# Transposes of x moved inside the first product, one load of x set back, and a new way out for the last rows

## The chip, the cores and the metric

The kernel runs on one core of one Trainium2 chip. The metric is device time in microseconds, from launch to end, as the median of several runs. The engines of the core are named as the profile names them: PE is TensorE (matmuls; PEld is its weight load), DVE is VectorE, ACT is ScalarE, POOL is GpSimd, SP is SyncE, which here only issues transfers. Each engine has a queue of its own and works through it in order. Transfers (DMAs) are issued from the queues of SP, ACT and POOL and run on the core's 16 DMA engines. SBUF is the on-chip memory of 128 partitions, PSUM the eight banks into which PE writes.

## The reference

One step of a hybrid decoder layer, with a prompt of 256 rows and 8 samples of 8 rows (64 sample rows) that share the weights. The model width is 2048, all in float32.

```python
def decoder_layer(x, conv_prev, k_win, v_win, rel_bias, w_in, w_conv, w_conv_out, sinks,
                  w_attn_out, w_o, g_mix, g_ffn, w_gate, w_up, w_down):
    xn = rms_norm(x, g_mix)
    z = xn @ w_in                       # B | C | h | q | k | v | gate_conv | gate_attn
    ...
    u = c_gate * h_conv
    conv_out, conv_state = short_conv(u, conv_prev, w_conv)
    y_conv = (b_gate * conv_out) @ w_conv_out
    ...                                 # banded attention with a bias and a sink per head
    y_attn = attn @ w_attn_out
    merged = jax.nn.sigmoid(gate_c) * y_conv + jax.nn.sigmoid(gate_a) * y_attn
    h = x + merged @ w_o
    hn = rms_norm(h, g_ffn)
    h = h + (jax.nn.silu(hn @ w_gate) * (hn @ w_up)) @ w_down
    return h, conv_state, k_state, v_state
```

After the layer comes a final RMSNorm: each row of h is divided by the root of its mean square and multiplied by `g_final`. The outputs are `y_prompt` (256 x 2048), `y_sample` (64 x 2048) and the new key, value and convolution states, for which the sample caches are copied on, shifted by 8 rows.

## The kernel before

All 320 rows are handled together, transposed: a matrix of activations lies in SBUF as 16 chunks of 128 features by 320 rows. Every float32 product is made of three matmuls. Weights and activations are each split into a high part (`hi`, `xh`, rounded to the format of the fast matmul) and the rest (`lo`, `xl`), and hi x xh, hi x xl and lo x xh are added up in PSUM. A tile of weights comes in by one transfer from SP's queue into `wraw` (four buffers), ACT makes `whi` (L93) and DVE `wlo` (L94), with three buffers each.

The framework orders each engine's queue by itself, from what is ready in its own plan, with the order of the program as priority; it also sets all semaphores. `with after(mark):` adds one rule: the instructions inside are queued behind `mark` on the same engine. It is an order and not a wait for data.

**Start.** x is loaded as rows: two tiles of 128 prompt rows and one of 64 sample rows (`xs`), in five groups of columns (`XB`, 2, 2, 4, 4 and 4 chunks; `x_load(i)` issues three transfers, from SP's queue but for one). The first product (`kv_product`, L267) makes keys and values and transposes x on the way. It takes 16 chunks in nine tiles of weights, two of one chunk and seven of two, and four groups of 128 columns, c = 0 to 3, so that a chunk costs twelve matmuls. `x_prep(kc)` (L242) transposes chunk kc of the three row tiles on PE into one PSUM bank; then ACT writes `xh`, DVE writes `xl` and copies x to `hT`. The splits of a weight tile are queued behind the `xh` and `xl` of its first chunk (L263). Chunks 0 and 1 are prepared ahead of the products of chunk 0, chunks 2 and 3 ahead of those of chunk 1, and from chunk 2 on, chunk kc + 2 ahead of the products of chunk kc. The loads of x are issued behind those of weight tiles: group 1 behind tile 0, group 2 behind tile 1, group 3 behind tile 3, group 4 behind tile 4.

After each tile, `tick()` places a piece of side work (`start_rest`, L321): small loads on POOL, the squares of x on ACT (`squares`, L314, three activations a time, four times), and small transposes and matmuls on PE. The products that follow (`product`, L116) take two column groups at a time and all 16 chunks, four to a tile of weights.

Among the loads for the first of these, the query product, the sample caches are copied from memory to memory (L417), by two transfers from SP's queue of which each counts 8 samples outermost.

**End.** The last product (`dn`) adds to `hT`. In its second half each pair of chunks is transposed back to rows, into PSUM banks (`pc`, "fa"), one bank a chunk with three row tiles side by side. ACT squares them and adds up along the row (`row_squares`, L908, into `ssf`), DVE multiplies by `g_final` into `y_sb`. For the last pair the first chunk (`next_last`, L923) is treated while PE still works on the second; there DVE also sums the squares so far (`s15`, L932 and L933). The last chunk is added to `hT` and transposed in three pieces by row tile (L966 and L967), into one bank. Then, for row tile 0 and afterwards for tiles 1 and 2, the last squares, the mean (`row_mean`, L969), the root (`inv_root`, L181), the scaling of all columns, split between ACT and DVE, and the sends. Five sends of prompt rows go from SP's queue. Two sends of the sample rows (columns 0 to 767 and 768 to 2047, from 64 partitions) go from ACT's queue; the code's last lines are

```python
    with after(last["a"]):
        scale(nc.scalar, 2, r2, 0, 768)
    send(nc.scalar, 2, 0, 768)
    with after(last["y"]):
        last["y"] = scale(nc.vector, 2, r2, 768, e0)
    with after(last["y"]):
        scale_last(2, r2)
    send(nc.scalar, 2, 768, D)
```

## Time and profile before

| | us |
|---|---|
| median of 3 runs (1702.07 to 1702.84) | 1702.33 |
| the profiled execution | 1702.27 |
| its span | 1700.5 |
| PE busy | 1682.2 |
| DVE busy | 863.3 |
| ACT busy | 643.5 |
| mean granted clock of PE | 0.997 |

The span runs from the first to the last instruction that the profile shows; the device time holds a little more around it. In a row of the timeline the columns are start, duration, engine, line of the kernel, operation, output and inputs with their shapes, and a count; brackets hold the idle time of the engine before it and what ended that. `SPq` and `ACTq` are the queues that issue transfers. In a row of waits stand the one who waits, what it waited for, and the sum, the number and the longest of the waits. In a row of transfers stand the destination and source, the issuing queue, the count, the size of each and the median time from issue to landing. In a row of windows stand the stretch, its length, the busy time of PE, PEld, DVE, ACT and POOL with their instructions, the granted clock, the busy share of the DMA engines and GB/s. Matmuls are pipelined and their ends are modelled.

### The profile page before, as it was taken

The numbers are of one execution on the slowest core, as the hardware profiler recorded it, in microseconds if no ns is written. First come the engines' busy times: TensorE is split into PE (matmuls) and PEld (weight loads), VectorE is DVE, ScalarE is ACT, GpSimd is POOL, SyncE is SP. The second block draws the span as 40 slices with busy tenths as digits, with TensorE's granted clock in tenths as the row PEclk, the third lists the DMA queues.
The fourth block names the chain that finished last, engine by engine and source line by source line (L and its number), as shares of the span: only waits on it lengthen the run. The fifth ranks groups of instructions, "written<-read, shape, count | busy, mean of one in ns | idle before, by whom it ended". The sixth has DMA issues, their size and how long they took to land.

```text
span 1700.5 us, 27713 instructions
## 1 busy us (share of the span) xinstructions
PE 1682.2 (99%) x11600; PEld 1670.9 (98%) x11600; DVE 863.3 (51%) x1231; ACT 643.5 (38%) x945; POOL 81.3 (5%) x127
## 2 busy tenths in 40 slices
PE   8999999999999999999999999999999999999996
PEld 7999999999999999999999999999999999999996
DVE  7667554444444445556454545433345545454443
ACT  6445443333333333334333333322233333333432
POOL 1001221000000001220000000000000000000000
PEclk9999999999999999999999999999999999999998
DMA  7754554555555544444444444444444444445442
GB/s 217 216 153 142 161 151 131 147 150 151 151 152 151 149 149 149 149 149 149 149 149 150 149 150 152 152 152 150 149 150 149 149 149 149 149 151 171 149 140 96
DMA packets 256719, 258.22 MB, mean 152 GB/s; under 512 B 9091, under 2 KB 251615, under 8 KB 256433
## 3 DMA queue, kind: packets, MB, share of 16 engines
q1 hardware_dynamic: 254128, 249.86, 47.8%
q0 software_dynamic: 2128, 5.92, 1.2%
q8 instruction: 91, 1.49, 0.4%
q10 hardware_dynamic: 336, 0.66, 0.2%
q14 instruction: 36, 0.29, 0.1%
HBM read 253.29 MB, written 5.08 MB: 152 GB/s over the span
## 4 chain that ended last, share of the span: by engine, by line
PE 95%; issue 2%; DMA 1%; DVE 1%; SPq 0%; POOL 0%; ACT 0%; DVEq 0%; POOLq 0%; ACTq 0%
PE fg L134 18%; PE fu L134 18%; PE dn L134 18%; PE wo L134 7%; PE ga L134 7%; PE gc L134 7%; PE C L134 3%; PE B L134 3%; PE H L134 3%; PE ya L134 3%; PE yc L134 3%; PE q L134 2%; DMA wraw<-in_w_in_dram 0%; DMA rel<-in_rel_bias_dram 0%; PE po L508 0%
## 5 line engine op out<-in xcount | busy, mean ns | idle before, releaser
L94 DVE TENSOR_TENSOR wlo<-wraw,whi 128x1024 fp32r<-128x1024 f32 (+1 forms) x481 | 573.8, 1195 | 703.9 <-ACT whi L93 701.3
L93 ACT ACTIVATE whi<-wraw 128x1024 fp32r<-128x1024 f32 (+1 forms) x481 | 493.3, 1030 | 852.4 <-PE dn L134 198.2
L134 PE MATMUL dn<-a_h,whi 128*128 128x320 f32 x704 | 218.5, 310 | 0.0
L134 PE MATMUL fu<-hh_t,whi 128*128 128x320 f32 x704 | 217.4, 309 | 0.0
L134 PE MATMUL dn<-a_h,wlo 128*128 128x320 f32 x704 | 217.3, 309 | 0.0
L134 PE MATMUL dn<-a_l,whi 128*128 128x320 f32 x704 | 217.2, 309 | 0.0
L134 PE MATMUL fg<-hh_t,whi 128*128 128x320 f32 x704 | 217.2, 309 | 0.0
L134 PE MATMUL fg<-hl_t,whi 128*128 128x320 f32 x704 | 217.2, 309 | 0.0
L134 PE MATMUL fg<-hh_t,wlo 128*128 128x320 f32 x704 | 217.2, 309 | 0.0
L134 PE MATMUL fu<-hl_t,whi 128*128 128x320 f32 x704 | 217.2, 308 | 0.0
L134 PE MATMUL fu<-hh_t,wlo 128*128 128x320 f32 x704 | 217.2, 308 | 0.0
L134 PEld LDWEIGHTS fu<-hl_t,whi 128*128 128x128 f32 x704 | 132.2, 188 | 0.1
L134 PEld LDWEIGHTS dn<-a_l,whi 128*128 128x128 f32 x704 | 132.2, 188 | 0.0
L134 PEld LDWEIGHTS fu<-hh_t,whi 128*128 128x128 f32 x704 | 132.2, 188 | 0.1
L134 PEld LDWEIGHTS dn<-a_h,whi 128*128 128x128 f32 x704 | 132.2, 188 | 0.0
L134 PEld LDWEIGHTS dn<-a_h,wlo 128*128 128x128 f32 x704 | 132.2, 188 | 0.0
L134 PEld LDWEIGHTS fg<-hh_t,whi 128*128 128x128 f32 x704 | 132.2, 188 | 0.0
L134 PEld LDWEIGHTS fg<-hh_t,wlo 128*128 128x128 f32 x704 | 132.2, 188 | 0.0
L134 PEld LDWEIGHTS fg<-hl_t,whi 128*128 128x128 f32 x704 | 132.2, 188 | 0.0
L134 PEld LDWEIGHTS fu<-hh_t,wlo 128*128 128x128 f32 x704 | 132.2, 188 | 0.0
L134 PE MATMUL gc<-xh_t,whi 128*128 128x320 f32 x256 | 79.6, 311 | 0.0
L134 PE MATMUL ga<-xh_t,wlo 128*128 128x320 f32 x256 | 79.4, 310 | 0.0
(285 smaller groups left out, 2934.7 us busy)
## 6 DMA issues: line engine op xcount, KB each, us to landing
wraw<-in_w_in_dram SPq DMA_DIRECT2D x119, 512.0 KB, 3.6
wraw<-in_w_gate_dram SPq DMA_DIRECT2D x88, 512.0 KB, 3.6
wraw<-in_w_up_dram SPq DMA_DIRECT2D x88, 512.0 KB, 3.6
wraw<-in_w_down_dram SPq DMA_DIRECT2D x88, 512.0 KB, 3.5
wraw<-in_w_o_dram SPq DMA_DIRECT2D x32, 512.0 KB, 3.5
wraw<-in_w_in_dram SPq DMA_DIRECT2D x34, 256.0 KB, 4.4
wraw<-in_w_conv_out_dram SPq DMA_DIRECT2D x16, 512.0 KB, 3.5
wraw<-in_w_attn_out_dram SPq DMA_DIRECT2D x32, 256.0 KB, 4.1
```

The lines of the kernel that those rows point to most:

```text
L93: last["hi"] = nc.scalar.activation(hi, src, AF.Copy)
L94: last["lo"] = nc.vector.tensor_sub(lo, src, hi.bitcast(F32))
L134: last["mm"] = nc.tensor.matmul(ps[c][:, :T], w[:, k, c * P:(c + 1) * P], x(kc), start=(kc == 0 and i == 0), stop=(kc == nk - 1 and i == 2),)
```

## The change

At the start, chunks 0 and 1 are prepared ahead of the first load of weights in the program, and every later chunk kc + 2 is prepared at c = 3 of chunk kc, with its transposes queued behind the matmuls issued so far (those of c = 0 to 2). Group 2 of x is loaded behind weight tile 2 instead of tile 1.

At the end, the last chunk's three transposes go to three PSUM banks; the sum of the squares so far is made behind the last adds. The sample rows are scaled into a new tile `yo` of 128 partitions by 1024 columns: columns 0 to 1023 of row r in partition r, columns 1024 to 2047 in partition 64 + r. ACT scales the first half, DVE the second. Two sends take 512 columns each of all 128 partitions; the destination's access pattern counts 2 halves, 64 rows and 512 columns. All sends go from SP's queue. The tile `yb` becomes larger by 1024 columns.

```diff
--- before.py
+++ after.py
@@ -241,8 +241,9 @@
 
     def x_prep(kc):
         pt = ps_aux(u("pt"))
-        for t in range(3):
-            nc.tensor.transpose(pt[:, t * P:(t + 1) * P], xs[t][:, kc * P:(kc + 1) * P], ident)
+        with after(*((last["mm"],) if kc > 1 else ())):
+            for t in range(3):
+                nc.tensor.transpose(pt[:, t * P:(t + 1) * P], xs[t][:, kc * P:(kc + 1) * P], ident)
         m1 = nc.scalar.activation(xh_t[:, kc, :], pt[:, :T], AF.Copy, scale=g_mix[:, kc:kc + 1])
         m2 = nc.vector.scalar_tensor_tensor(
             xl_t[:, kc, :], pt[:, :T], g_mix[:, kc:kc + 1], xh_t[:, kc, :].bitcast(F32),
@@ -267,6 +268,8 @@
     def kv_product(tiles, x_after):
 
         ps = [ps_acc(u("kv")) for _ in range(4)]
+        x_prep(0)
+        x_prep(1)
         k0 = 0
         for i, n in enumerate(tiles):
             hi, lo = load_kv(k0, n)
@@ -277,9 +280,8 @@
                 order.sort(key=lambda kc: kc[1])
             for k, c in order:
                 kc = k0 + k
-                if c == 0:
-                    for j in range(2 * kc, 2 * kc + 2) if kc < 2 else range(kc + 2, min(kc + 3, KC)):
-                        x_prep(j)
+                if c == 3 and kc + 2 < KC:
+                    x_prep(kc + 2)
                 for m, (w, x) in enumerate(((hi, xh), (hi, xl), (lo, xh))):
                     last["mm"] = nc.tensor.matmul(
                         ps[c][:, :T], w[:, k, c * P:(c + 1) * P], x(kc),
@@ -363,7 +365,7 @@
         nc.vector.tensor_mul(rbsq, rb, rb)
 
     side_work[0] = start_rest()
-    ps_kv = kv_product([1, 1] + [2] * 7, {0: (1,), 1: (2,), 3: (3,), 4: (4,)})
+    ps_kv = kv_product([1, 1] + [2] * 7, {0: (1,), 2: (2,), 3: (3,), 4: (4,)})
     for _ in side_work[0]:
         pass
     for c in range(2):
@@ -897,9 +899,11 @@
                 split_to(a_h[:, fpair * 2 + c, :], a_l[:, fpair * 2 + c, :], gs[c])
         if half == 1:
             ya = xp.tile([P, 2, D], F32, tag="xh", name="ya")
-            yb = xp.tile([P, 2, D], F32, tag="xl", name="yb")
-            y_sb = [ya[:, 0, :], ya[:, 1, :], yb[:, 0, :]]
-            gfb = yb[:, 1, :]
+            yb = xp.tile([P, 2 * D + DC], F32, tag="xl", name="yb")
+            y_sb = [ya[:, 0, :], ya[:, 1, :], yb[:, 0:D]]
+            gfb = yb[:, D:2 * D]
+
+            yo = yb[:, 2 * D:]
             nc.gpsimd.dma_start(gfb, a["g_final"].partition_broadcast(P))
             ssf = op.tile([P, 3, KC], F32, name="ssf")
             nc.vector.memset(ssf, 1.0)
@@ -908,14 +912,21 @@
             def row_squares(t, k, pt):
                 tn = TOK[t][1]
                 jk = tmp("td", "jk")
-                nc.scalar.activation(
-                    jk[:tn, :P], pt[:tn, t * P:(t + 1) * P], AF.Square, accum_out=ssf[:tn, t, k:k + 1]
-                )
+                nc.scalar.activation(jk[:tn, :P], pt[t][:tn], AF.Square, accum_out=ssf[:tn, t, k:k + 1])
 
             def y_part(k, pt):
                 for t, (t0, tn) in enumerate(TOK):
                     ks = slice(k * P, (k + 1) * P)
-                    nc.vector.tensor_mul(y_sb[t][:tn, ks], pt[:tn, t * P:(t + 1) * P], gfb[:tn, ks])
+                    nc.vector.tensor_mul(y_sb[t][:tn, ks], pt[t][:tn], gfb[:tn, ks])
+
+            def to_rows(k, dst, tr=(0, 1, 2)):
+                for t in tr:
+                    t0, tn = TOK[t]
+                    nc.tensor.transpose(dst[t][:tn], hT[:, k, t0:t0 + tn], ident)
+
+            def one_bank():
+                pt = ps_aux(u("fa"))
+                return [pt[:, t * P:(t + 1) * P] for t in range(3)]
 
             warm = op.tile([P, 1], F32, name="warm")
             with after(last["sig"]):
@@ -923,14 +934,11 @@
         def next_last(ps):
 
             k = KC - 2
-            pc[0] = ps_aux(u("fa"))
+            pc[0] = one_bank()
             nc.vector.tensor_add(hT[:, k, :], hT[:, k, :], ps[0][:, :T])
-            for t, (t0, tn) in enumerate(TOK):
-                nc.tensor.transpose(pc[0][:tn, t * P:(t + 1) * P], hT[:, k, t0:t0 + tn], ident)
+            to_rows(k, pc[0])
             for t in range(3):
                 row_squares(t, k, pc[0])
-            nc.vector.tensor_reduce(s15, ssf[:, :, 0:KC - 1], axis=AX.X, op=ALU.add)
-            nc.vector.tensor_scalar(s15, s15, 1.0 / D, EPS, op0=ALU.mult, op1=ALU.add)
 
         pc = [None, None]
         for mp in range(8):
@@ -946,11 +954,9 @@
                 k = mp * 2 + c
                 nc.vector.tensor_add(hT[:, k, :], hT[:, k, :], ps[c][:, :T])
             if half == 1:
-                pc = [ps_aux(u("fa")) for _ in range(2)]
+                pc = [one_bank() for _ in range(2)]
                 for c in range(2):
-                    k = mp * 2 + c
-                    for t, (t0, tn) in enumerate(TOK):
-                        nc.tensor.transpose(pc[c][:tn, t * P:(t + 1) * P], hT[:, k, t0:t0 + tn], ident)
+                    to_rows(mp * 2 + c, pc[c])
                 for c in range(2):
                     k = mp * 2 + c
                     for t in range(3):
@@ -959,12 +965,15 @@
 
 
     e0 = (KC - 2) * P
-    pc[1] = ps_aux(u("fa"))
+    pc[1] = [ps_aux(u("fa"))[:, 0:P] for _ in range(3)]
     k = KC - 1
     for t, (t0, tn) in enumerate(TOK):
         tr = slice(t0, t0 + tn)
-        nc.vector.tensor_add(hT[:, k, tr], hT[:, k, tr], ps[1][:, tr])
-        nc.tensor.transpose(pc[1][:tn, t * P:(t + 1) * P], hT[:, k, tr], ident)
+        last["h"] = nc.vector.tensor_add(hT[:, k, tr], hT[:, k, tr], ps[1][:, tr])
+        to_rows(k, pc[1], (t,))
+    with after(last["h"]):
+        nc.vector.tensor_reduce(s15, ssf[:, :, 0:KC - 1], axis=AX.X, op=ALU.add)
+        last["s"] = nc.vector.tensor_scalar(s15, s15, 1.0 / D, EPS, op0=ALU.mult, op1=ALU.add)
 
     def row_mean(ts):
         vf = op.tile([P, ts.stop - ts.start], F32, name=u("vf"))
@@ -973,62 +982,74 @@
         )
         return vf
 
-    def rows(t):
-        return y_p[0, t * P:(t + 1) * P, :] if t < 2 else y_s.flatten_outer_dims()
+    def to_send(t, a0, a1):
+        if t < 2:
+            return y_sb[t][:, a0:a1]
+        h = a0 // DC
+        return yo[h * 64:h * 64 + 64, a0 - h * DC:a1 - h * DC]
 
     def scale(eng, t, r, a0, a1):
-        y = y_sb[t][:TOK[t][1], a0:a1]
+        tn = TOK[t][1]
+        y, z = y_sb[t][:tn, a0:a1], to_send(t, a0, a1)
         if eng is nc.scalar:
-            return nc.scalar.activation(y, y, AF.Copy, scale=r[:TOK[t][1]])
-        return nc.vector.tensor_scalar(y, y, r[:TOK[t][1]], None, op0=ALU.mult)
+            last["a"] = nc.scalar.activation(z, y, AF.Copy, scale=r[:tn])
+        else:
+            last["y"] = nc.vector.tensor_scalar(z, y, r[:tn], None, op0=ALU.mult)
 
     def scale_last(t, r):
         tn = TOK[t][1]
         for c in range(2):
-            ks = slice(e0 + c * P, e0 + (c + 1) * P)
+            a0 = e0 + c * P
             last["y"] = nc.vector.scalar_tensor_tensor(
-                y_sb[t][:tn, ks], pc[c][:tn, t * P:(t + 1) * P], r[:tn], gfb[:tn, ks], op0=ALU.mult, op1=ALU.mult
+                to_send(t, a0, a0 + P), pc[c][t][:tn], r[:tn], gfb[:tn, a0:a0 + P], op0=ALU.mult, op1=ALU.mult
             )
 
-    def send(eng, t, a0, a1):
-        eng.dma_start(rows(t)[:, a0:a1], y_sb[t][:TOK[t][1], a0:a1])
+    def send(t, a0, a1):
+        if t < 2:
+            return nc.sync.dma_start(y_p[0, t * P:(t + 1) * P, a0:a1], y_sb[t][:, a0:a1])
+        ys = y_s.flatten_outer_dims()
+        nc.sync.dma_start(
+            bass.AP(ys.tensor, ys.offset + a0, [[DC, 2], [D, 64], [1, a1 - a0]]), yo[:, a0:a1]
+        )
 
     row_squares(0, k, pc[1])
-    r0 = inv_root(row_mean(slice(0, 1)), [P, 1], "rf", op)
+    with after(last["s"]):
+        v0 = row_mean(slice(0, 1))
+    r0 = inv_root(v0, [P, 1], "rf", op)
     with after(last["root"]):
         for t in (1, 2):
             row_squares(t, k, pc[1])
     with after(last["inv"]):
-        first = scale(nc.vector, 0, r0, 0, 256)
-    send(nc.sync, 0, 0, 256)
+        scale(nc.vector, 0, r0, 0, 256)
+    send(0, 0, 256)
     with after(last["root"]):
         scale(nc.scalar, 0, r0, 256, 1024)
-    send(nc.sync, 0, 256, 1024)
-    with after(first):
+    send(0, 256, 1024)
+    with after(last["y"]):
         scale_last(0, r0)
     with after(last["y"]):
         v12 = row_mean(slice(1, 3))
     with after(last["v"]):
-        last["y"] = scale(nc.vector, 0, r0, 1024, e0)
-    send(nc.sync, 0, 1024, D)
-    with after(last["y"]):
+        scale(nc.vector, 0, r0, 1024, e0)
+    send(0, 1024, D)
+    with after(last["y"], last["a"]):
         r12 = inv_root(v12, [P, 2], "rf", op)
-    with after(last["inv"]):
-        r1, r2 = r12[:, 0:1], r12[:, 1:2]
-        last["a"] = scale(nc.scalar, 1, r1, 0, 640)
-        send(nc.sync, 1, 0, 640)
-        last["y"] = scale(nc.vector, 1, r1, 640, e0)
+    r1, r2 = r12[:, 0:1], r12[:, 1:2]
+    with after(last["inv"], last["root"]):
+        scale(nc.scalar, 1, r1, 0, 640)
+        scale(nc.vector, 1, r1, 640, e0)
+    send(1, 0, 640)
     with after(last["y"]):
         scale_last(1, r1)
-    send(nc.sync, 1, 640, D)
+    send(1, 640, D)
     with after(last["a"]):
-        scale(nc.scalar, 2, r2, 0, 768)
-    send(nc.scalar, 2, 0, 768)
+        scale(nc.scalar, 2, r2, 0, DC)
     with after(last["y"]):
-        last["y"] = scale(nc.vector, 2, r2, 768, e0)
+        scale(nc.vector, 2, r2, DC, e0)
+    send(2, 0, 512)
     with after(last["y"]):
         scale_last(2, r2)
-    send(nc.scalar, 2, 768, D)
+    send(2, 512, DC)
 
 
 _INS = ['x_prompt', 'x_sample', 'cache_k', 'cache_v', 'state_conv', 'rel_bias', 'w_in', 'w_conv',
```

## The prediction

> **What bounds the kernel.** I read the page's busy times and its chain first, then TensorE's waits over the whole run. The page's lines say that TensorE (PE) fills the span and that the chain is 95% PE.
>
> ```profile
> span 1700.5 us, 27713 instructions
> ...
> PE 1682.2 (99%) x11600; PEld 1670.9 (98%) x11600; DVE 863.3 (51%) x1231; ACT 643.5 (38%) x945; POOL 81.3 (5%) x127
> ...
> PE 95%; issue 2%; DMA 1%; DVE 1%; SPq 0%; POOL 0%; ACT 0%; DVEq 0%; POOLq 0%; ACTq 0%
> ```
>
> The view of waits, for PE alone over the whole run, after its first wait, which is for the engine's own warm-up data (total, times, longest):
>
> ```profile
> PE pt L245 <- DMA x<-in_x_sample_dram: 1.5, 1, 1.5
> PE kv L284 <- ACT whi L93: 1.2, 1, 1.2
> PE kv L284 <- DVE wlo L94: 0.8, 1, 0.8
> PE fa L967 <- DVE hT L966: 0.6, 1, 0.6
> ```
>
> All lie in the first 17 us or the last 14. Between them PE works without a stop, so a microsecond won at the start arrives at the end; and behind PE's last transpose only the output path counts. The change touches these two ends. The profiled execution took 1702.27 us, 1.77 more than its span and 0.06 under the median 1702.33. A difference of 0.2%, 3.4 us, is about the least that a measurement of this kernel tells from none.
>
> **The start.** The timeline:
>
> ```profile
> 4.54 0.91 SPq L228 DMA_DIRECT2D x<-in_x_prompt_dram  x2
> ...
> 5.91 0.93 ACT L246 ACTIVATE xh_t<-pt,vecs 128x320 fp32r<-128x320 f32 x2
> 6.00 1.10 SPq L258 DMA_DIRECT2D wraw<-in_w_in_dram  x2
> ...
> 8.03 0.33 PE L245 MATMUL pt<-ident,x 128*128 128x128 f32 x1 [1.48 <-DMA x<-in_x_sample_dram]
> ...
> 8.11 0.83 PE L284 MATMUL kv<-xh_t,whi 128*128 128x320 f32 x4
> 8.58 0.63 ACT L93 ACTIVATE whi<-wraw 128x512 fp32r<-128x512 f32 x1 [1.75 <-DMA wraw<-in_w_in_dram]
> ...
> 10.20 0.40 PE L284 MATMUL kv<-xh_t,whi 128*128 128x320 f32 x1
> ...
> 12.67 1.06 ACT L93 ACTIVATE whi<-wraw 128x1024 fp32r<-128x1024 f32 x1 [3.04 <-DMA wraw<-in_w_in_dram]
> ...
> 13.78 0.41 PE L284 MATMUL kv<-xh_t,whi 128*128 128x320 f32 x1 [1.24 <-ACT whi L93]
> ...
> 15.04 1.22 DVE L94 TENSOR_TENSOR wlo<-wraw,whi 128x1024 fp32r<-128x1024 f32 x1
> ```
>
> Two more rows: the stage behind it by windows (last two columns: DMA share, GB/s), and one stretch of the chain:
>
> ```profile
> 12.00:14.00 2.00, 0.76 (x6) 0.52 (x5) 0.00 (x0) 1.33 (x2) 0.00 (x0) 1.00 1.06 390
> ```
>
> ```profile
> 343.32 14.08 PE gc L134 x96
> ```
>
> A product takes 14.08 / 96 = 0.147 us. PE's queue holds the transposes of chunk 2 ahead of the products of chunk 0, and waits until 8.03 for sample rows, although chunk 0 is ready at about 6.4 (first half of the ACT row at 5.91). After the change these transposes stand behind nine of chunk 0's twelve products, so the products run from 6.5. Chunk 1 then starts when its weights do, 8.58 + 0.63 = 9.21, instead of 10.20: a lead of 1.0 us.
>
> Next, chunk 2. Its weights (512 KB, the first of the two issues at 6.00) waited in SP's queue behind the third load of x. Setting that load back lets them go at 4.54, 1.46 us earlier. They then land between 12.67 - 1.46 = 11.2, if nothing else changes, and 9.9, if their 512 KB run at 390 GB/s straight behind the tile that ended the wait at 8.58. The products of chunk 2 start 1.1 us after landing (13.78 less 12.67), and not before chunk 1 is through, 9.21 + 2.1 = 11.3: at 11.3 to 12.3 against 13.78, a gain of 1.5 to 2.5 us. The load of x that is set back is 640 KB; it is first needed at the end of chunk 2, past 13 us, and would end about when these weights end now, 12.6. It is hidden; if it came 1 us late PE would wait that 1 us. The loads behind keep their places, and POOL's small loads, which wait for chunk 3's xh, move with it.
>
> The wait for wlo (0.8) stays: its place on VectorE (DVE), behind chunk 3's x work, is not touched. I take 2.0 us for the start, the middle of 1.5 and 2.5, with 3.5 (all three waits gone) as the upper end.
>
> What can take it back is that the other transposes are also moved nine products later:
>
> ```profile
> 22.95 0.49 PE L245 MATMUL pt<-ident,x 128*128 128x128 f32 x3
> ...
> 24.85 0.62 ACT L317 ACTIVATE junk<-x 128x512 f32<-128x512 f32 x1
> 24.98 1.23 DVE L94 TENSOR_TENSOR wlo<-wraw,whi 128x1024 fp32r<-128x1024 f32 x1
> 25.04 0.49 PE L245 MATMUL pt<-ident,x 128*128 128x128 f32 x3
> ...
> 27.73 0.40 PE L284 MATMUL kv<-xh_t,whi 128*128 128x320 f32 x1
> ```
>
> The split of a weight tile is queued behind the x work of its first chunk. From the transposes at 22.95 to the end of wlo, 26.21, are 3.26 us, and the tile is used at 27.73: covered. A chunk takes 2.09 (22.95 to 25.04), twelve products of 0.147 and 0.33 for transposes. Nine products later, 0.33 + 3 x 0.147 + 2.09 = 2.86 us are left until the tile's first product and 0.3 more until the first that reads wlo: 0.1 late, in each of six tiles, 0.6 in all. It is zero where a side matmul fills the gap or the products with whi go first, as they did at 13.78. So the gain is between 3.5 and 1.5 - 1.0 = 0.5, and I leave 2.0.
>
> **The end, up to the first output.** The timeline:
>
> ```profile
> 1686.76 0.20 DVE L932 TENSOR_REDUCE s<-ssf 128x3 f32<-128x45 f32 x1 [1.68 <-ACT jk L911]
> 1686.88 0.28 DVE L966 TENSOR_TENSOR hT<-hT,dn 128x128 f32<-128x128 f32 x1
> 1687.07 0.16 DVE L933 TENSOR_SCALAR s<-s 128x3 f32<-128x3 f32 x1
> 1687.14 0.41 DVE L966 TENSOR_TENSOR hT<-hT,dn 128x128 f32<-128x128 f32 x2
> ...
> 1687.21 0.70 PE L967 MATMUL fa<-ident,hT 128*128 128x128 f32 x3 [0.57 <-DVE hT L966]
> 1688.01 0.28 ACT L911 ACTIVATE jk<-fa 128x128 f32<-128x128 f32 x1 [1.28 <-PE fa L967]
> ...
> 1688.41 0.16 DVE L971 SCALAR_TENSOR_TENSOR vf<-ssf,s 128x1 f32<-128x1 f32 x1 [0.86 <-ACT jk L911]
> ```
>
> The reduction leaves the place ahead of the first add: the add starts 0.12 earlier. With a bank for each transpose the first square need not wait for the third: one transpose is a third of the 0.70, so ACT starts about 0.43 earlier. The mean at 1688.41 comes at 1687.86. The moved reduction and scaling, 0.36, now begin when the adds end, 1687.55 - 0.12 = 1687.43, and end at 1687.8: hidden by 0.07; without that cover they cost up to 0.36. I take 0.55, bounds 0.2 and 0.7. The rest of the chain, root and scales, keeps its steps, and every send of the prompt rows goes 0.55 earlier.
>
> **The end, sample rows.** SP's last wait, behind that for the prompt rows (ya), and two stages by windows:
>
> ```profile
> SPq L1069 <- DMA out_dram<-yb: 2.2, 1, 2.2
> ```
>
> ```profile
> 1695.00:1696.00 1.00, 0.00 (x0) 0.00 (x0) 0.00 (x0) 0.00 (x0) 0.00 (x0) 0.50 1.06 422
> 1697.00:1698.00 1.00, 0.00 (x0) 0.00 (x0) 0.00 (x0) 0.00 (x0) 0.00 (x0) 0.50 1.09 227
> ```
>
> The sample rows (512 KB) land 2.2 us after the prompt rows. From 64 partitions they move at 227 GB/s, the prompt rows from 128 at 422, with the engines full in both. The new sends read 128 partitions, in runs of 2 KB. But their destination counts two halves outermost, then 64 rows. The kernel has a transfer of that kind: the cache copies (L417), whose outermost count is the 8 samples, 960 KB each in pieces of 60 KB. Pages of the DMA view of three stretches in a row (49.75 to 52, 50.3 to 52.05, 52.05 to 54.4), and two landings, of the weight load before the copies and of that issued behind them:
>
> ```profile
> DMA packets 38, 0.50 MB, mean 223 GB/s; under 512 B 8, under 2 KB 30, under 8 KB 30
> ...
> DMA packets 22, 0.01 MB, mean 6 GB/s; under 512 B 0, under 2 KB 22, under 8 KB 22
> ...
> DMA packets 259, 0.62 MB, mean 262 GB/s; under 512 B 9, under 2 KB 251, under 8 KB 251
> ```
>
> ```profile
> wraw<-in_w_in_dram SPq DMA_DIRECT2D x2, 256.0 KB, 3.8
> ...
> wraw<-in_w_in_dram SPq DMA_DIRECT2D x1, 256.0 KB, 12.5
> ```
>
> Eight large packets start, none for 1.75 us, then eight more: the copies ran on eight engines, 0.49 MB in 2.3 us or 26.7 GB/s each, and a load behind them took 12.5 us instead of 3.8. By this the new sends, which count 2, run on two engines, one for each half: 2 x 64 x 2 KB = 262 KB apiece. For the pace I take 24.4 GB/s, 390 / 16, of the row at 12 us, where x and weights come in runs of 2 KB: 10.7 us in place of 2.2, **+8.5 us**. Ends: 9.8 us at the copies' 26.7; 18.5 at 227 / 16 = 14.2, the pace where two engines share a path. No row shows which side's count decides where they differ, 128 here against 2; that is the second rival.
>
> The Trainium skill, "DMA: Bandwidth & Descriptors", section "Why a DMA increments its semaphore by 16 and not by 1", says that the engines used are the largest number up to 16 that divides the outermost counts of both sides; by that rule, two here. The trace agrees for 8 against 8.
>
> The longer scale on ACT (768 to 1024 columns), the shorter one on DVE and the two issues moved from ACT's queue to SP's lie under the prompt rows' transfer, which still fills the engines at 1695. Nothing waits for ACT after them.
>
> **Sum.** 1702.27 - 2.0 - 0.55 + 8.5 = **1708.2 us**.
>
> **Rivals.**
> *Sixteen engines* (other side): the source's 128 partitions decide, and 524 KB go at 390 GB/s in 1.3 us, 0.9 less than now. 1702.27 - 2.0 - 0.55 - 0.9 = 1698.8. For it: the 422 of the prompt sends, 128 against 128. Against it: the copies ran eight packets at a time, and their only eight is the outermost count. It decides from five engines up: 524 KB at 122 GB/s take 4.3 us, 2.1 more than now, less than the 2.55 gained. The Trainium skill, "SBUF — State Buffer", section "Door 1: The DMA port swizzle", holds that 64 partitions reach 8 of 16 ports; by it alone this rival would be the forecast, and 227 against 422 agrees.
> *The lead too short*: an ACT square (0.62, at 24.85) stands ahead of xh in each of the four tiles that have squares. With the 0.1 in six tiles that is 4 x 0.62 + 0.6 = 3.1 on top: 1711.3. Against it: the squares now start behind the tile's split and not ahead of it.
> *Two engines at the slow pace*, 18.5 us: 1716.0. Against it: the two halves lie 64 partitions apart.
>
> **How the numbers follow.** Two engines at the taken pace 0.78; sixteen 0.13; short lead 0.06; slow pace 0.03. The first alone spans 1705.9 (copies' pace, 1.3 more at the start, 0.15 at the mean) to about 1710.1 (start 0.5, mean 0.2). With the short lead included, 1704.8 to 1712.2 holds 8 in 10. Slower 0.87; the second rival, at 3.5 us, splits into 0.08 faster and 0.05 same.
>
> **What would show it.** Between the landings of ya and yb, SP's wait should be near 10.7 instead of 2.2, and the DMA share of the last 10 us about 2/16. PE's wait for the sample rows should be gone, that for whi shorter, and the q products should start 2 us earlier. The mean of the first rows should come 0.5 us sooner after the last product. I am wrong if the last stage shows a full DMA share, or if kv products wait for wlo in most tiles.

## The result and the profile after

The changed kernel takes **1710.6 us** (median of 6 runs, 1710.39 to 1710.93). The kernel before, run beside it, takes 1702.38 (1702.02 to 1702.84). The ratio is 1.0049, 95% interval 1.0036 to 1.0062: slower by 8.2 us. The prediction said 1708.2, 1704.8 to 1712.2, slower with a chance of 0.87. Sign, size and mechanism came out as forecast; one term of the sum, the start, was too large.

The page of the changed kernel. Its profiled execution took 1710.55 us, 1.85 more than its span (1.77 before).

```profile
span 1708.7 us, 27715 instructions
...
PE 1684.1 (99%) x11600; PEld 1671.7 (98%) x11600; DVE 863.9 (51%) x1231; ACT 643.8 (38%) x945; POOL 81.3 (5%) x127
...
PE 98%; DVE 1%; DMA 0%; ACT 0%; SPq 0%; issue 0%; DVEq 0%; ACTq 0%
```

PE's busy time grew by 1.9 us, and no engine's by more, so the busy times do not name a loss of 8.2. It lies behind the last computation. PE's waits over the whole run, after the first one, which is as before (total, times, longest):

```profile
...
PE kv L286 <- DVE wlo L94: 0.7, 1, 0.7
PE fa L925 <- DVE hT L972: 0.4, 1, 0.4
```

The waits for sample rows (1.5) and for whi (1.2) are gone, as they should be. A wait for wlo remains, but not the one of before: it is now at 36.65, not at 16.31. SP's wait at the end, the last stretches by windows (last two columns: DMA share, GB/s) and the issues of the sample sends:

```profile
SPq L1090 <- DMA out_dram<-yb: 12.6, 2, 7.5
```

```profile
1696.00:1698.00 2.00, 0.00 (x0) 0.00 (x0) 0.00 (x0) 0.00 (x0) 0.00 (x0) 0.50 0.10 26
1698.00:1700.00 2.00, 0.00 (x0) 0.00 (x0) 0.00 (x0) 0.00 (x0) 0.00 (x0) 0.50 0.13 51
...
1704.00:1706.00 2.00, 0.00 (x0) 0.00 (x0) 0.00 (x0) 0.00 (x0) 0.00 (x0) 0.50 0.13 51
```

```profile
1692.67 1.98 SPq L1011 DMA_DIRECT2D out_dram<-yb  x2
```

SP has issued the last sample send at 1692.67 + 1.98 = 1694.65 and waits 12.6 in two pieces, to 1707.25. The prompt rows have drained by about 1696. No engine computes any more, and from 1698 on the transfers run at a share of 0.13, which is 2 of 16, and at 51 GB/s, 25.6 for each of two. With the landing of ya put at 1696, that of yb comes 11.25 us behind it instead of 2.2: **+9.05** against the 8.5 of the sum.

The chain up to the first output, in the timeline:

```profile
1686.08 0.62 DVE L972 TENSOR_TENSOR hT<-hT,dn 128x128 f32<-128x128 f32 x3 [1.60 <-PE dn L134]
1686.42 0.64 PE L925 MATMUL fa<-ident,hT 128*128 128x128 f32 x3 [0.38 <-DVE hT L972]
...
1686.84 0.17 DVE L976 TENSOR_SCALAR s<-s 128x3 f32<-128x3 f32 x1
1686.84 0.28 ACT L915 ACTIVATE jk<-fa 128x128 f32<-128x128 f32 x1 [0.72 <-PE fa L925]
...
1687.24 0.16 DVE L980 SCALAR_TENSOR_TENSOR vf<-ssf,s 128x1 f32<-128x1 f32 x1 [0.24 <-ACT jk L915]
```

The mean starts at 1687.24 instead of 1688.41, 1.17 earlier. The start of the kernel brings 0.6 of that (below); the chain brings the other **0.57**. The first square starts 0.42 after the first transpose; before, it started 0.80 after. These 0.38 come from the bank of its own (0.43 were forecast). The rest, about 0.2, is the first add: it starts 0.04 behind the last product, before 0.24 (0.12 were forecast).

### The profile page after: what moved, and what is told of

It reads as the page before. It is cut to its first block, busy times and chain, and to the rows that moved or that the text cites. A ratio compares the mean times of both kernels' runs of the same rounds, so it can differ in the third digit from the quotient of the medians.

```text
span 1708.7 us, 27715 instructions
## 1 busy us (share of the span) xinstructions
PE 1684.1 (99%) x11600; PEld 1671.7 (98%) x11600; DVE 863.9 (51%) x1231; ACT 643.8 (38%) x945; POOL 81.3 (5%) x127
## 4 chain that ended last, share of the span: by engine, by line
PE 98%; DVE 1%; DMA 0%; ACT 0%; SPq 0%; issue 0%; DVEq 0%; ACTq 0%
PE dn L134 18%; PE fu L134 18%; PE fg L134 18%; PE wo L134 7%; PE gc L134 7%; PE ga L134 7%; PE C L134 3%; PE B L134 3%; PE H L134 3%; PE ya L134 3%; PE yc L134 3%; PE q L134 3%; PE kv L286 2%; PE po L510 0%; PE fa L925 0%; PE pp L497 0%
## 5 line engine op out<-in xcount | busy, mean ns | idle before, releaser
L134 PE MATMUL ga<-xh_t,whi 128*128 128x320 f32 x256 | 79.5, 310 | 0.0
```

Source lines behind the costliest of these rows:

```text
L134: last["mm"] = nc.tensor.matmul(ps[c][:, :T], w[:, k, c * P:(c + 1) * P], x(kc), start=(kc == 0 and i == 0), stop=(kc == nk - 1 and i == 2),)
```

## The experiments

### The sends undone

The changed kernel, with the sample rows scaled in place and sent from 64 partitions as before; start and chain stay.

```diff
-        h = a0 // DC
-        return yo[h * 64:h * 64 + 64, a0 - h * DC:a1 - h * DC]
+        return y_sb[t][:TOK[t][1], a0:a1]
...
-    send(2, 0, 512)
+    send(2, 0, 768)        # on ACT's queue, from y_sb[2][:64]
...
-    send(2, 512, DC)
+    send(2, 768, D)
```

> The changed kernel with the sample rows scaled in place and sent as before (64 partitions, columns 0 to 767 and the rest, on ACT's queue); start and chain of the mean stay as changed. Theory (the new sends run on two DMA engines, and that is the whole loss): the last landing comes about 2.2 us after that of the prompt rows instead of 11.25, so 1710.6 - 9.05 = 1701.5 us, or 1702.4 - 0.6 (start) - 0.6 (chain) = 1701.2. Rival (the loss lies in the start, the chain or the longer span of products, and the sends only look slow because they come last): stays above 1706.

Measured: 1701.45 us (before, in this and the next three comparisons, 1702.67); ratio 0.9993, interval 0.9983 to 1.0003. SP's last waits are back in their old form:

```profile
SPq L1084 <- DMA out_dram<-ya: 3.3, 1, 3.3
SPq L1084 <- DMA out_dram<-yb: 2.2, 1, 2.2
```

So the rest of the change is worth 1.22 us, near the 0.59 + 0.57 that the trace of after gives, and too little to be told from none with certainty. The whole loss is in the sends.

### The sends alone

The kernel before, with nothing but the new scaling and the new sends.

```diff
+        ys = y_s.flatten_outer_dims()
+        eng.dma_start(
+            bass.AP(ys.tensor, ys.offset + a0, [[DC, 2], [D, 64], [1, a1 - a0]]), yo[:, a0:a1]
+        )
...
+    send(nc.sync, 2, 0, 512)
...
+    send(nc.sync, 2, 512, DC)
```

> The kernel before with nothing but the new sends (scaled into the spare columns, 128 partitions, counts 2 x 64, SP's queue). Theory: +9 us on the kernel before, 1711.4 us; DMA share in the last 9 us 2/16 = 0.125. Rival (the loss needs the moved transposes or the other banks): 1702.4, within 1 us.

Measured: 1711.66 us, **+8.99**; ratio 1.0055, interval 1.0040 to 1.0070. A window late in its transfer and SP's wait read as in the changed kernel:

```profile
1704.00:1706.00 2.00, 0.00 (x0) 0.00 (x0) 0.00 (x0) 0.00 (x0) 0.00 (x0) 0.50 0.13 51
```

```profile
SPq L1082 <- DMA out_dram<-yb: 12.6, 2, 7.5
```

The cost does not need the other parts. The two runs sum to +8.99 - 1.22 = 7.8; the whole change measures 8.2.

### The destination's counts

Three kernels change only how the destination of the sample rows is counted. Source, bytes, pieces of 2 KB and queue stay as in the changed kernel. The blocks land in another order, so these three kernels leave the rows of the sample output permuted: their times show what the counts cost, and they are no versions to use.

```diff
-            bass.AP(ys.tensor, ys.offset + a0, [[DC, 2], [D, 64], [1, a1 - a0]]), yo[:, a0:a1]
+            bass.AP(ys.tensor, ys.offset + a0, [[DC, 128], [1, a1 - a0]]), yo[:, a0:a1]
```

> The changed kernel with the destination of the sample rows counted in one run of 128 blocks of 4 KB instead of 2 x 64: the same bytes in the same 2 KB pieces from the same 128 partitions on the same queue, but the blocks land in another order, so the rows of the sample output are permuted. Theory (the outermost count of the destination sets the number of engines): sixteen engines, the sends of 512 KB in 1.3 us at about 390 GB/s instead of 10.25, so the last landing 1 to 2 us after the prompt rows': 1710.6 - 9.5 = 1701 us. Rival 1 (pieces of 2 KB into rows, or 128 source partitions, are slow in themselves): stays at 1710.6. Rival 2 (SP's queue holds the sample sends behind the prompt sends): stays within 2 us of 1710.6.

Measured: **1700.51 us**, 10.1 less than the changed kernel; ratio to before 0.9988, interval 0.9979 to 0.9997. The engines stay full to the end:

```profile
1695.00:1696.00 1.00, 0.00 (x0) 0.00 (x0) 0.00 (x0) 0.00 (x0) 0.00 (x0) 0.50 0.94 357
```

```profile
1695.30:1696.50 1.20, 0.00 (x0) 0.00 (x0) 0.00 (x0) 0.00 (x0) 0.00 (x0) 0.50 1.00 381
```

Neither the 2 KB pieces, nor the 128 source partitions, nor SP's queue is at fault. How the destination is counted decides 10 us.

Then eight runs outermost, with steps under which both counts make one run of blocks:

```diff
+            bass.AP(ys.tensor, ys.offset + a0, [[16 * DC, 8], [DC, 16], [1, a1 - a0]]), yo[:, a0:a1]
```

> The changed kernel with the destination of the sample rows counted 8 x 16 blocks of 4 KB instead of 2 x 64 (the rows of the sample output are permuted as with one run of 128). Theory: eight engines, 65.5 KB on each at 25.6 GB/s = 2.6 us instead of 10.25, so 1710.6 - 7.7 = 1702.9 us, DMA share near 0.5 while they run. Rival 1 (any count below 16 falls back to one or two engines): 1710.6. Rival 2 (only the bytes and pieces count): as one run of 128, about 1701.

Measured: 1700.57 us, not 1702.9: rival 2's figure. But the reading was not forced: 8 runs of 16 blocks, end to end, are 128 blocks in a row, and such a pattern may be joined on the way to the transfer. So the counts were kept and the steps exchanged, so that they cannot be joined:

```diff
+            bass.AP(ys.tensor, ys.offset + a0, [[DC, 8], [8 * DC, 16], [1, a1 - a0]]), yo[:, a0:a1]
```

> The changed kernel with the destination of the sample rows counted 8 x 16, the eight runs one block apart and the sixteen eight blocks apart, so that the two counts cannot be read as one run of 128, as those of the 8 x 16 run before could (it took as long as one run of 128: 1700.57 against 1700.51 us; the rows of the sample output are permuted). Theory (engines = outermost count): eight engines hold all 512 KB, 65.5 KB each at 25.6 GB/s = 2.6 us, beside the last of the prompt rows; 1701.5 to 1703 us, and a stretch of 1 to 2 us with a DMA share near 0.5. Rival (any split count falls back to two engines): 1710.6 us.

Measured: **1703.56 us** beside 1702.52, ratio 1.0005, interval 0.9995 to 1.0015; 0.6 above the range expected. The windows:

```profile
1695.00:1696.00 1.00, 0.00 (x0) 0.00 (x0) 0.00 (x0) 0.00 (x0) 0.00 (x0) 0.50 0.97 372
1696.00:1697.00 1.00, 0.00 (x0) 0.00 (x0) 0.00 (x0) 0.00 (x0) 0.00 (x0) 0.50 0.51 53
1697.00:1698.00 1.00, 0.00 (x0) 0.00 (x0) 0.00 (x0) 0.00 (x0) 0.00 (x0) 0.50 0.47 152
1698.00:1699.00 1.00, 0.00 (x0) 0.00 (x0) 0.00 (x0) 0.00 (x0) 0.00 (x0) 0.50 0.52 174
```

As soon as the prompt rows are out, the share stands near 0.5, eight of sixteen. The sample rows begin slowly, as in the changed kernel: 53 GB/s from 1696 to 1697. Then they move 152 and 174 GB/s, 19 to 22 for each engine, less than the 25.6 taken for the estimate. Both make the sends longer than expected. But the 0.6 is not theirs alone: this execution also holds a wait of 0.59 for wlo in the query product, which the trace of the changed kernel does not have.

A second count of the engines does not use the busy share. The DMA view was asked for the stretch behind the prompt rows' packets, in which only the two sample sends run. Beside the 2 KB packets of the rows it lists a few under 512 B. In this order: the changed kernel (1695.75 to 1708.7), 8 x 16 apart (1696.35 to 1701.6), 8 x 16 joined (1695.8 to 1698.7), one run of 128 (1695.35 to 1698.2).

```profile
DMA packets 256, 0.52 MB, mean 40 GB/s; under 512 B 4, under 2 KB 4, under 8 KB 256
```

```profile
DMA packets 257, 0.49 MB, mean 94 GB/s; under 512 B 16, under 2 KB 16, under 8 KB 257
```

```profile
DMA packets 262, 0.47 MB, mean 162 GB/s; under 512 B 32, under 2 KB 32, under 8 KB 262
```

```profile
DMA packets 247, 0.44 MB, mean 155 GB/s; under 512 B 32, under 2 KB 32, under 8 KB 247
```

For each of the two sends these are 2, 8, 16 and 16, the same numbers of engines as the shares give. So the engines follow the outermost count of the destination, taken after such joining: 2, 8 and 128, where the source's is 128 each time.

The Trainium skill, "DMA: Bandwidth & Descriptors", section "Why a DMA increments its semaphore by 16 and not by 1", takes the largest number up to 16 that divides both sides' outermost counts, as the instruction carries them, and for transfers of this kind the lowest-numbered engines. The runs agree with the number: 0.13, 0.5 and a full share. The second part fits too: both sends of the changed kernel had been issued by 1694.65, and the share stayed at 0.13, as it would if they share the same two engines. The traces do not number the engines.

### Why the start brought 0.6 and not 2.0

First, where the gain went in the trace of the changed kernel. Chunk 2's products do start 2.2 earlier than before (13.78), and the q products behind the first product only 0.59 earlier (45.76 before):

```profile
11.60 0.40 PE L286 MATMUL kv<-xh_t,whi 128*128 128x320 f32 x1
...
18.09 0.49 PE L246 MATMUL pt<-ident,x 128*128 128x128 f32 x3
...
33.91 0.49 PE L246 MATMUL pt<-ident,x 128*128 128x128 f32 x3
...
36.65 0.42 PE L286 MATMUL kv<-xh_t,wlo 128*128 128x320 f32 x1 [0.70 <-DVE wlo L94]
...
37.79 0.49 PE L246 MATMUL pt<-ident,x 128*128 128x128 f32 x3
...
45.17 0.31 PE L134 MATMUL q<-xh_t,whi 128*128 128x320 f32 x1
```

The same places in the kernel before:

```profile
18.76 0.49 PE L245 MATMUL pt<-ident,x 128*128 128x128 f32 x3
...
34.22 0.49 PE L245 MATMUL pt<-ident,x 128*128 128x128 f32 x3
...
37.00 0.55 PE L245 MATMUL pt<-ident,x 128*128 128x128 f32 x3
...
45.76 0.31 PE L134 MATMUL q<-xh_t,whi 128*128 128x320 f32 x1
```

The transposes of one chunk can be followed through both kernels; those of before stand nine products (1.32 us) nearer the front. The transposes of chunk 6 come at 18.09, before at 18.76 + 1.32 = 20.08: 1.99 ahead, just the 2.0 of the prediction. Up to the q products 1.40 of it is lost. Between the transposes of chunks 13 and 14 alone lie 3.88 us instead of 2.78. ACT's row at that place:

```profile
32.35 0.53 ACT L247 ACTIVATE xh_t<-pt,vecs 128x320 fp32r<-128x320 f32 x1 [0.83 <-PE pt L246]
32.89 1.28 ACT L185 ACT_TABLE_LOAD   x1
34.18 0.20 ACT L185 ACTIVATE r<-r 128x3 f32<-128x3 f32 x1
34.30 1.04 ACT L93 ACTIVATE whi<-wraw 128x1024 fp32r<-128x1024 f32 x1
```

The root for r3 needs another table of functions. Its load stands between xh of chunk 12 and the split of the tile that waits behind that xh. It stood at 33.20 in the kernel before too:

```profile
33.20 1.28 ACT L185 ACT_TABLE_LOAD   x1
```

But there the transposes ran nine products further ahead, and nothing waited. Two experiments on this, each one edit of the changed kernel. The table first:

```diff
     nc.vector.memset(ones, 1.0)
+    nc.scalar.activation(cst.tile([P, 1], F32, name="warm0"), ones[:, 0:1], AF.Sqrt)
```

> The changed kernel with one dummy root on ACT right after its first memset, so that the table with the root is loaded at the start of the kernel, where ACT waits for weights, and not at 32.89 between xh and whi of chunks 12 and 13. Theory (the shorter lead lets that load of 1.28 us through to PE): the wait for wlo at 36.65 (0.70 shown, 0.87 against the pace of the matmuls) is gone, the q products start 0.9 earlier, 44.3 instead of 45.17, time 1709.7 us. Rival (the wait comes from DVE's own queue or from the transposes, and stays): q products at 45.2, 1710.6 us.

Measured: q products at 44.37, 0.80 earlier; 1710.45 us (the kernel before took 1702.52 beside it and beside the other kernels below, where no other figure stands). ACT loads the table once, at 1.18, where it has nothing else to do:

```profile
1.18 1.28 ACT L159 ACT_TABLE_LOAD   x1 [1.18 <-PEq L1083]
```

```profile
32.53 0.53 ACT L248 ACTIVATE xh_t<-pt,vecs 128x320 fp32r<-128x320 f32 x1 [0.86 <-PE pt L247]
32.95 0.19 ACT L186 ACTIVATE r<-r 128x3 f32<-128x3 f32 x1
```

The wait for wlo is gone and most of the forecast 0.9 came: the trace shows the theory right. The median time fell by less than 0.2, within the spread of the runs; the span of the profiled execution fell by 0.6. A load of a table costs 1.28 here with nothing else around it. The Trainium skill, "ScalarE: Activation LUTs", section "What ACT_TABLE_LOAD costs", has the same 1283 ns and adds a drain of about 1.38 us; here xh ends at 32.88, the load starts at 32.89, and the root follows 0.01 us behind it, so the traces do not show the second part.

Then the transposes earlier:

```diff
-                if c == 3 and kc + 2 < KC:
+                if c == 1 and kc + 2 < KC:
```

> The changed kernel with the transposes of chunk kc+2 put ahead of the second of chunk kc's four column blocks and not ahead of the fourth, 6 products or 0.9 us earlier. Theory (the lead of the transposes is too short for xh, whi and wlo behind it): the waits for wlo at 36.65 (0.87) and the four gaps of 0.16 in the tiles before go, q products start 1.5 earlier, 43.7 instead of 45.17, time 1709.1 us. Rival (the lead is not the cause; ACT and DVE are as late whenever the transposes come): q products at 45.2, 1710.6 us; if the transposes then wait for x, later than that.

Measured: q products at 44.05, 1.12 earlier, not 1.5; 1710.15 us. The gaps ahead of wlo are gone (0.16 at 16.96 and at 21.40 in the changed kernel), but a wait of 0.56 for wlo came up at chunk 1, whose split on DVE is queued behind the x work of chunk 2, which now comes earlier:

```profile
11.59 0.41 PE L286 MATMUL kv<-xh_t,wlo 128*128 128x320 f32 x1 [0.56 <-DVE wlo L94]
```

Then the other part of the start alone: the transposes at c = 3, with the load of x put back to its old place.

```diff
-    ps_kv = kv_product([1, 1] + [2] * 7, {0: (1,), 2: (2,), 3: (3,), 4: (4,)})
+    ps_kv = kv_product([1, 1] + [2] * 7, {0: (1,), 1: (2,), 3: (3,), 4: (4,)})
```

> The changed kernel with group 2 of x loaded behind weight tile 1 again; the transposes stay where the change put them. Theory (the start's gain is the earlier issue of chunk 2's weights; the transposes only cost lead): chunk 2's products start at 13.3 to 13.8 instead of 11.60, and without a lead to lose the wait behind the table load shrinks or goes; q products at 45.8 to 46.3 instead of 45.17, no earlier than the 45.76 of the kernel before, time 1711.2 to 1711.7 us. Rival (the moved transposes bring the start's gain by themselves): q products at 45.2, 1710.6 us.

Measured: **1714.62 us** (before 1703.22), ratio 1.0068, interval 1.0051 to 1.0085; q products at 48.41. Both theories missed, by 2 us and more. Chunk 2 starts when the theory said; then the timeline, and two stretches by windows (the third column from the end is PE's granted clock):

```profile
13.83 0.63 PE L286 MATMUL kv<-xh_t,whi 128*128 128x320 f32 x1 [2.08 <-ACT whi L93]
14.27 0.47 PE L286 MATMUL kv<-xl_t,whi 128*128 128x320 f32 x1
...
21.34 0.49 PE L246 MATMUL pt<-ident,x 128*128 128x128 f32 x3
...
39.89 0.41 PE L286 MATMUL kv<-xh_t,wlo 128*128 128x320 f32 x1 [0.70 <-DVE wlo L94]
```

```profile
11.75:13.75 2.00, 0.00 (x1) 1.00 1.04 382
13.90:17.10 3.20, 3.20 (x13) 0.50 1.03 309
```

Two things had been left out. PE gets through chunks 0 and 1 faster here and then waits 2.08 in one piece for chunk 2's weights, where the kernel before waits 1.48 and 1.24 in two. Behind the 2.08 the granted clock is 0.50 for at least the 3.2 us of this stretch, and the products stand 0.27 apart instead of 0.147. The Trainium skill, "TensorE: Matmul & The Clock Gate", section "Part 1: The HAM clock gate (the "warmup" mystery)", has the half clock and a window of about 3.4 us; the 3.2 or more at half clock are near it, while its idle window of about 3.4 is longer than the wait that sufficed here.

And the wait behind the table load is as long as before, although there is no time won ahead of it. The transposes of chunk 6 come at 21.34, 1.26 behind those of the kernel before (20.08 at the same place), which is the slow stretch; the q products come 2.65 behind, so 1.39 are lost between the two, as 1.40 were in the changed kernel. That loss does not depend on how early the stage starts. It is the chain xh, (table load), whi, wlo, less the cover from a chunk's transposes to the first product that reads wlo, and the place in PE's queue sets this cover. I had taken the time won ahead of chunk 2 for a reserve that the chain uses up; it is none, because the chain begins with PE's own transposes. So the parts of the start have opposite signs: with the transposes late, the load of x is worth 48.41 - 45.17 = 3.2 us, 2.2 of wait and 1 of clock; the late transposes cost 1.4 in both kernels. The times say the same: this kernel is 11.4 slower than the kernel before beside it, the changed kernel 8.2.

### A faster version

The sample rows in two parts that count 64 outermost on both sides, the rest as in the changed kernel:

```diff
+        h = a0 // DC
+        eng = nc.sync if h else nc.scalar
+        eng.dma_start(y_s.flatten_outer_dims()[:, a0:a1], yo[h * 64:h * 64 + 64, a0 - h * DC:a1 - h * DC])
...
+    send(2, 0, DC)
...
+    send(2, DC, D)
```

> The changed kernel with the sample rows sent in two parts that each count 64 rows outermost on both sides: columns 0 to 1023 from partitions 0 to 63 on ACT's queue, the others from partitions 64 to 127 on SP's. Theory: sixteen engines for each part, both halves of the partitions read at once, so about 390 GB/s as with one run of 128 blocks: 1700.5 us, the last landing 0.5 to 1.5 us after that of the prompt rows. Rival (a part reads 64 partitions only, and each goes at 227 GB/s, one after the other): as the sends from 64 partitions before, 1701.4 us.

Measured: 1701.26 us, ratio 0.9993, interval 0.9984 to 1.0002: the figure of the rival. Behind the prompt rows the engines are full at a low rate:

```profile
1696.00:1697.00 1.00, 0.00 (x0) 0.00 (x0) 0.00 (x0) 0.00 (x0) 0.00 (x0) 0.50 0.95 251
1697.00:1698.00 1.00, 0.00 (x0) 0.00 (x0) 0.00 (x0) 0.00 (x0) 0.00 (x0) 0.50 0.97 287
```

The DMA view by queue (q10 is ACT's, q1 SP's), for 1696.5 to 1697 and for 1697.5 to 1698, shows what these rates are made of:

```profile
DMA packets 26, 0.11 MB, mean 213 GB/s; under 512 B 0, under 2 KB 0, under 8 KB 26
...
q10 hardware_dynamic: 23, 0.09, 86.7%
```

```profile
DMA packets 55, 0.18 MB, mean 361 GB/s; under 512 B 11, under 2 KB 11, under 8 KB 55
...
q1 hardware_dynamic: 46, 0.18, 93.7%
```

The two parts go one behind the other, so 128 partitions are not read at once. ACT's part, from partitions 0 to 63, moves 213 GB/s, close to the 227 that 64 partitions gave before; SP's part, from 64 to 127, then moves 361. So a send from 64 partitions is not always held to 227; why the second is faster, no run shows.

Three more on top of it: with the dummy root and the transposes at c = 1; the same with partitions 64 to 127 sent in two parts; and that with c = 2. The first:

> The sample rows sent in two parts of 64 rows (as in the run with two halves, 1701.26 us, q products at 45.27), the dummy root first, and the transposes of chunk kc+2 ahead of chunk kc's second column block. Theory: the two start edits share a cause (the lead), so their gains of 0.80 and 1.12 do not add up; the transposes moved up leave about 0.3 for the table load. q products at 43.8, time 1701.26 - 1.45 = 1699.8 us, faster than before by 0.16%. Rival (they add up): q products at 43.3, 1699.3 us.

Measured: **1699.86 us**, ratio 0.9983, interval 0.9974 to 0.9992; q products at 44.25. The time is as expected and is below both kernels by more than its interval, though not by the 0.2% named in the prediction. The q products are no earlier than with c = 1 alone (44.05), so the gains of the two edits overlap wholly: the table load is covered once the transposes come early. Against the run with two halves alone the start brings 1.0 and the time falls by 1.4. The trace of the run with two halves also has a wait of 0.94 for wlo in the query product, at 65.37, which the trace here lacks; apart from that the difference is within the spread.

```diff
-        scale(nc.vector, 2, r2, DC, e0)
+        scale(nc.vector, 2, r2, DC, 1536)
+    send(2, DC, 1536)
+    with after(last["y"]):
+        scale(nc.vector, 2, r2, 1536, e0)
```

> As the run before it, with the half of partitions 64 to 127 sent in two parts (columns 1024 to 1535 as soon as DVE has scaled them), so that both halves of the partitions are read while the last prompt rows drain, in place of 251 and 287 GB/s in the last 2 us of the run with two halves. Theory: 0.4 us less than the run before it, 1699.4 us. Rival (one more issue of 0.5 us on SP and one more operation on DVE cost what it brings): the same, 1699.8 us.

Measured: 1700.03 us, ratio 0.9983, interval 0.9975 to 0.9992: the same; the finer sends bring nothing.

> As the run before it, with the transposes ahead of the third column block, 0.44 later than ahead of the second. Theory (the lead counts up to where nothing waits any more; with the table load gone only the gaps of 0.16 and the first tiles are left): q products within 0.3 of 43.8, time within 0.3 us of the run before it. Rival (each 0.44 of lead is worth 0.44 of time): 0.4 us more.

Measured: 1700.3 us, ratio 0.9985, interval 0.9976 to 0.9994; q products at 44.34 against 44.01. Time and products are 0.3 later than with c = 1. That is between theory and rival, and within the scatter: kernels with the same start have their q products anywhere from 45.05 to 45.58. It decides nothing.

## Why the prediction was right, and where not

| term | predicted | measured |
|---|---|---|
| start (q products) | -2.0 | -0.59 |
| chain to the first mean | -0.55 | -0.57 |
| sample sends | +8.5 | +9.05 (trace), +8.99 (alone) |
| sum | +5.9 | +7.9; profiled executions +8.28 |

- **Sample sends: right, shown.** Two engines, at 25.6 GB/s each instead of the 24.4 taken, a little faster: 10.25 us and not 10.7 for the 524 KB. That the term still came out 0.5 larger lies in the window from 1696 to 1698, at 26 GB/s and not 51, which costs 1.0: the two engines do not take up the sample rows at full pace as soon as the prompt rows drain. Why, no run shows. The evidence from the cache copies, eight packets at a time, carried over to 128 against 2, and the run with 8 against 128 fills in the middle.
- **Chain: right.** 0.57 against 0.55. The moved reduction ends at 1687.01, ahead of the mean at 1687.24: hidden, as said.
- **Start: mis-sized**, 2.0 against 0.59, near the lower bound of 0.5. That this bound held has some luck in it: it takes off 1.0, for which the working has only 0.6 of late tiles, and the other kernels with the same start have their q products between 45.05 and 45.58, a gain of 0.2 to 0.7. The step for the load of x held: chunk 2's products came 2.2 earlier, within 1.5 to 2.5, and at chunk 6 1.99 of it stood. (The lead ahead of it was smaller than said: chunk 1 started at 9.79 and not at 9.21, 0.4 earlier than before instead of 1.0. The sum did not use it.) The step that failed is the cover of the later transposes: "0.1 late, in each of six tiles", 0.6 in all as an end, with 2.0 left as the value taken. The late tiles without a table load came near it, 0.16 at 16.96 and at 21.40. But the tile of chunks 12 and 13 alone lost 1.10 (3.88 against 2.78), because the chain priced there (xh, whi, wlo) left out the table load that ACT has between them; with that load moved to the start of the kernel, 0.80 came back. The timeline of the kernel before showed that load at 33.20, covered; the prediction never asked what stood in the chain in other tiles than the one it measured.
- **The wait for wlo** was said to stay. That of chunk 2 went, and a new one of 0.70 came behind the table load.
- **The rivals.** Sixteen engines would have been 1698.8; the run with 128 outermost shows that case at 1700.5, and the missing 1.4 of the start accounts for most of the difference. "It decides from five engines up" was too kind: with eight the kernel took 1703.56, no faster than before, though part of that lies outside the sends. The short lead was the right worry with the wrong cause: not squares of ACT ahead of xh, but the table load behind it, and 1.4 us, not 3.1. The slow pace of 14.2 GB/s did not occur.

The two misses, 1.4 at the start and 0.5 at the sends, point the same way, so the time came out 2.4 above the forecast and inside its range. Of the 0.4 between the terms and the profiled difference, 0.08 lies outside the span (1.85 against 1.77); the rest I could not place; it is no larger than the spread of the runs.

## What to carry to other kernels

When a transfer is re-cut so that it reads more partitions, look at the outermost count of both sides before the bandwidth: here a count of 2 left two of sixteen engines, and that cost 9 us where the rest of the change brought about 1.2. When a step moves later in an engine's queue, price its chain in every tile, with the one-off instructions that stand in it, and not in a typical one; a time won earlier is no reserve for a chain that begins behind the step itself. And a loss that lies behind the last instruction is seen in the windows' DMA share and in SP's last wait, not in the busy times.

## What was not expected of the hardware

Behind one wait of 2.08 us PE's granted clock stood at half for at least 3.2 us, while it stayed at full behind the waits of 1.48 and 1.24 in the kernel before; each is seen in one trace. So a wait in one piece can cost half as much again as its length: 1 us on 2.08 here. Counts of 8 x 16 ran like one of 128 where their steps joined them to one run (1700.57 and 1700.51 us), and like 8 where they did not (1703.56): what counts is the pattern after such joining, not as it is written; where the joining happens, no run shows. Eight engines wrote 19 to 22 GB/s each, two wrote 25.6 each; why the eight were slower, no run shows. And two sends of 64 partitions on two queues, from the two halves of the partitions, did not run at once: the lower half moved 213 GB/s, then the upper 361, while the sends of 128 partitions that were counted as one run moved 381.
